# Column projections written half by half, two more weight tiles, and PSUM banks in turn for the delta heads

## The chip, the cores and the metric

The kernel runs on one core of a Trainium2 chip. Its engines are TensorE (PE in the profile; its weight loads are listed apart as PEld), VectorE (DVE), ScalarE (ACT), GpSimd (POOL) and SyncE (SP), which here issues the DMAs. Each engine works through its own instruction list in order and waits on semaphores. TensorE writes its results into PSUM, which has eight banks of 128 x 512 floats; ACT and DVE read them out from there. The metric is the device time of one execution in microseconds (us), the median of three: 2317.09 us before the change, with 2314.77 as the lowest and 2318.42 as the highest.

## The reference

Two transformer-like layers are applied in turn to x, 1024 tokens of 1024 features, in float32. Cut to what the change touches:

```python
# first layer
proj = einsum('bld,de->ble', rmsnorm(x), w_in)          # 1024 x 4112
attn = neighbourhood_attention(aq, ak, av) * silu(az)   # 8 heads of 64, a window of 8 x 16 tokens
qkv  = silu(depthwise_conv(dq, dk, dv))                 # 4 delta heads of 128, five taps along the tokens
dq, dk = l2norm(dq), l2norm(dk)
a_mat = strict(kb @ k^T) * decay + I                    # per chunk of 64 tokens, both directions
intra = (q @ k^T) * decay
# ... triangular solve, a scan over chunks with a state, gate, then x = x + [attn, delta] @ w_out
# second layer
proj = einsum('bsd,dc->bsc', rmsnorm(x), w_in_2)        # 1024 x 10240
out_a = stick_breaking_attention(q, k, v) * silu(sb_g)  # 8 heads of 128
out_b = rmsnorm(chunkwise_retention(rot(r_q), rot(r_k), r_v)) * silu(r_g)   # 4 heads of 256
merged = sigmoid(m_sb) * (out_a @ w_branch_sb) + sigmoid(m_ret) * (out_b @ w_branch_ret)
x = x + merged @ w_out_2
```

## The kernel before

Every large product is done as three matmuls in a rounded format (fp32r): the activations are held as a high part and a low part, the weights too, and high x high, low x high and high x low are added in PSUM. The weights come from DRAM in tiles of 128 rows. `split_unit` (line 60) loads one such tile (`raw`), and GpSimd makes the high part of it (L70) and the low part (L71); some loads of the stage with eight attention heads give every second tile to ACT and DVE. `load_units` does this for the eight tiles of a weight panel up to 512 columns wide. The split tiles (`wu`) live in the pool `wpool` of 10 buffers, so beside the eight of the panel in use two of the next panel fit.

Two forms of projection use a panel. `dense_tok` (L102 for its matmuls) puts tokens on the partitions: one accumulator `acc` per 128 tokens. `dense_col` (L112) puts 128 output features on the partitions and all 1024 tokens on the free axis; these need two accumulators of 512 tokens. It takes two banks at once and writes matmuls to the two halves in turn: for each of the eight weight tiles and each of the three passes one matmul per half, 48 in all (the framework regroups some of them, as far as its two banks allow). `dense_half` (L120) does one half alone, 24 matmuls into one bank; before, only the very last block of the program uses it. The accumulators come from pool `psA`, three banks called "a". The other five banks are "z" (two), "t", "o" and "p".

The stages, in order, with what they are called in the profile's times:

- up to 57 us: the first norm, the transposes and one `dense_tok`;
- 57 to 320 us, delta heads (loop at L296): for each of four heads three columns by `dense_col` (q, k, v), each read out by ACT into `pad` (L315), convolved by five DVE instructions (L318, L320) and put through Silu (L323). Then small products on TensorE: sums of squares (L330), transposes of k and v (L341, L351) and of the normalized k (L355), k k^T (L402) and q k^T (L417). Each has a fixed bank tag: "z", "z", "t", "o", "t", "p". The results are weighted on DVE (`N`, `IT`, `sct`) and leave for DRAM;
- 320 to 610 us, neighbourhood attention of eight heads, beside a triangular solver on DVE and POOL;
- 610 to 850 us, the scan over chunks and the product with `w_out`;
- 850 to 1440 us, eight heads of stick-breaking attention: `dense_tok` of the next head beside the attention of the present one, one `dense_col` per head for the gate;
- 1440 to 1960 us, retention, four heads: `ret_proj` makes q and k by four columns, rotates them on DVE and POOL (L1103 to L1108), makes v by `dense_tok` and the gate by two columns; `ret_chain` makes scores (L1151), weights `wT`, a transposed and scaled k called `kd` (L132, L1162, L1163), outputs (L1171, L1179) and states (L1192) chunk by chunk;
- 1960 us to the end: the rest of the merge logits, two branch products and the last product, all by `dense_col`.

The program is written with one pool-and-tile framework that orders the instructions itself (`schedule_with_timeline_sim=True`): it places an instruction on its engine's list when its own estimate says that its inputs and its buffer are ready. So the order in which lines stand in the source is not the order on an engine, and a change of buffers moves instructions of all engines. `tbank(tags)` (line 159) takes the next tag of a string, in turn, through one counter for the whole program.

Of the kernel before, what the change touches and what calls it, by code (L numbers as in the profile page):

```python
# [19 lines left out]
P = 128  # L20
T = 1024
NM = 8
NK = 8
# [13 lines left out]
def tile_kernel(ctx: ExitStack, tc: tile.TileContext, I: dict, out: bass.AP, dbg=None, stop=None):  # L37
    nc = tc.nc
# [7 lines left out]
    wraw = ctx.enter_context(tc.tile_pool(name="wraw", bufs=3))  # L46
    wpool = ctx.enter_context(tc.tile_pool(name="wpool", bufs=10))
    psA = ctx.enter_context(tc.tile_pool(name="psA", bufs=3, space=PSUM))
# [57 lines left out]

    def dense_col(hT, us, c0):
        accs = [bank("a") for _ in range(2)]
        for k in range(NK):
            for i, (a, b) in enumerate(((0, 0), (1, 0), (0, 1))):  # L110
                for half in range(2):
                    nc.tensor.matmul(accs[half], lhsT=us[k][:, b, c0:c0 + P], rhs=hT[a][:, k, half * 512:(half + 1) * 512],  # L112
                                     start=(k == 0 and i == 0), stop=(k == NK - 1 and i == 2))
        return accs

    def dense_half(hT, us, c0, half):
        acc = bank("a")
        for k in range(NK):
            for i, (a, b) in enumerate(((0, 0), (1, 0), (0, 1))):
                nc.tensor.matmul(acc, lhsT=us[k][:, b, c0:c0 + P], rhs=hT[a][:, k, half * 512:(half + 1) * 512],  # L120
                                 start=(k == 0 and i == 0), stop=(k == NK - 1 and i == 2))
        return acc

    def rsqrt_small(dst, src, mul, eps, eshape):
# [179 lines left out]
    for h in range(4):  # L304
# [22 lines left out]
        nc.scalar.activation(out=sq, in_=sT[0], func=AF.Square)  # L327
        pq = bank("z")
        for m in range(NM):
# [7 lines left out]
        for g in range(2):  # L337
            pk = bank("z")
            for j in range(4):
                m = g * 4 + j  # L340
                nc.tensor.transpose(pk[:, j * P:(j + 1) * P], sT[1][:, m * P:(m + 1) * P], ident)  # L341
            for j in range(4):
# [4 lines left out]
                                    in1=ks[:, g * 4:g * 4 + 4].unsqueeze(2).to_broadcast([P, 4, P]), op=ALU.mult)  # L347
            pv = bank("t")
            for j in range(4):
                m = g * 4 + j  # L350
                nc.tensor.transpose(pv[:, j * P:(j + 1) * P], sT[2][:, m * P:(m + 1) * P], ident)  # L351
            nc.scalar.copy(out=vt[:, g * 4:g * 4 + 4, :].rearrange("p m d -> p (m d)"), in_=pv)
            pk2 = bank("o")
            for j in range(4):
# [12 lines left out]
        for d in range(2):  # L367
# [27 lines left out]
            else:  # L395
                E2 = decay(gb, G, 1, True, "E1")
                nc.vector.tensor_tensor(out=E2, in0=E2, in1=bb, op=ALU.mult)
                for g in range(2):
                    pkk = bank("t")
                    for j in range(4):  # L400
# [12 lines left out]
                for g in range(2):  # L413
                    pkq = bank("p")
                    for j in range(4):
                        n = g * 4 + j
                        nc.tensor.matmul(pkq[:, j * P:(j + 1) * P], lhsT=kT[:, n * P:(n + 1) * P],  # L417
                                         rhs=sT[0][:, n * P:(n + 1) * P], start=True, stop=True)
                    for dd_, E in enumerate((E0, E1)):
                        IT = dn.tile([P, 4, P], F32, tag="IN", name="IT", bufs=2)  # L420
                        nc.vector.tensor_tensor(out=IT, in0=pkq.rearrange("p (n c) -> p n c", n=4),
                                                in1=E[:, g * 4:g * 4 + 4, :], op=ALU.mult)
                        nc.sync.dma_start(out=d_pk[dd_, g * 4:g * 4 + 4, :, 3, h, :].rearrange("n p c -> p n c"), in_=IT)
# [842 lines left out]
    for q in range(2):  # L1266
        us = load_units(I["w_out_2"], q * 512, 512)
        for b in range(4):
            last = 4 * q + b == 7
            for half, acc in enumerate(dense_col(mgT, us, b * P) if not last else (dense_half(mgT, us, b * P, x) for x in range(2))):  # L1270
                hs = slice(half * 512, half * 512 + 512)
# [76 lines left out]
```

## Time and profile before

| | |
|---|---|
| median of three runs | 2317.09 us |
| the profiled execution | 2316.85 us, its span from first to last instruction 2315.1 us |
| TensorE's mean granted clock | 0.984 of full speed |
| TensorE matmuls (PE) | busy 2182.2 us, 94% of the span, 12197 instructions |
| weight loads (PEld) | busy 1875.5 us, 81%, 12197 instructions |
| DVE, ACT, POOL | busy 1242.6, 879.1 and 1210.2 us |
| DMA | 249.25 MB, 108 GB/s |

The profile is one execution seen by the hardware profiler. "Busy" is the time in which an engine has an instruction running; overlapping instructions count once. Matmuls are pipelined, so one matmul's listed duration (about 0.39 us for 512 columns) is longer than the distance to the next. A view of waits names the engine and line that waited, what released it, the total, the number of times and the longest one. The granted clock is the share of TensorE's full 2.4 GHz that the chip allowed in a stretch: it is either 1.0 or 0.5 (1.2 GHz).

### The profile page before, as it was taken

What the parts mean: (1) busy time and instruction counts of PE and PEld (TensorE: products, weight loads), DVE (VectorE), ACT (ScalarE), POOL (GpSimd) and SP (SyncE); (2) the same over time, 40 slices, a digit from 0 to 9 for tenths busy, and PEclk for the clock granted to TensorE, in tenths of its full rate; (3) what the DMA queues carried; (4) which work ended last, traced back from release to release, by engine and by line L of the source; (5) the groups of instructions that cost most, each with busy time, mean ns of one, the idle gap of its engine ahead of it and who ended that gap; (6) DMA issues with size and microseconds to landing.
All of it is one profiled execution on the core that took longest, in us unless ns stands there. A gap on an engine that the chain in (4) does not pass through costs nothing.

```text
span 2315.1 us, 33643 instructions
## 1 busy us (share of the span) xinstructions
PE 2182.2 (94%) x12197; PEld 1875.5 (81%) x12197; DVE 1242.6 (54%) x2228; ACT 879.1 (38%) x2191; POOL 1210.2 (52%) x1435
## 2 busy tenths in 40 slices
PE   7998888899999988999999999999989999999999
PEld 7777877787898778988888888788878788788887
DVE  4688789844457555665566453327474744321221
ACT  5344434445544225565566544012222222321200
POOL 6667778762004345554565545536575754434531
PEclk9999999999999999999999999999999999999999
DMA  4266830054486431110111103221324333644433
GB/s 129 83 165 166 206 86 26 35 159 130 146 280 215 147 106 42 55 47 23 51 51 55 51 32 97 67 69 55 125 87 132 95 105 101 218 164 152 142 106 107
DMA packets 238791, 249.25 MB, mean 108 GB/s; under 512 B 40032, under 2 KB 173856, under 8 KB 238368
## 3 DMA queue, kind: packets, MB, share of 16 engines
q1 hardware_dynamic: 238624, 247.10, 34.0%
q8 instruction: 96, 1.57, 0.3%
q14 instruction: 71, 0.58, 0.1%
HBM read 171.51 MB, written 75.53 MB: 107 GB/s over the span
## 4 chain that ended last, share of the span: by engine, by line
PE 43%; POOL 7%; DVE 7%; issue 4%; DMA 3%; ACT 3%; SPq 0%; POOLq 0%; ACTq 0%
PE acc L112 26%; PE acc L102 9%; PE acc L859 3%; POOL wu L71 2%; DMA raw<-in_w_in_dram 2%; PE po L1063 2%; DVE A L1042 1%; POOL wu L70 1%; DVE A L1037 1%; POOL A L1047 1%; PE pt L1179 1%; POOL ss L126 1%; ACT A L1036 1%; DVE xo L909 1%; DVE kf L132 1%
## 5 line engine op out<-in xcount | busy, mean ns | idle before, releaser
L112 PE MATMUL acc<-h2h,wu 128*128 128x512 f32 x1504 | 460.5, 396 | 0.7 <-POOL wu L71 0.4
L102 PE MATMUL acc<-wu,h2h 128*128 128x384 f32 (+1 forms) x1536 | 374.5, 326 | 11.5 <-DVE v L1117 5.5
L71 POOL TENSOR_TENSOR wu<-raw,wu 128x512 fp32r<-128x512 f32 (+3 forms) x268 | 364.9, 1370 | 6.1
L70 POOL TENSOR_SCALAR wu<-raw 128x512 fp32r<-128x512 f32 (+3 forms) x268 | 206.3, 773 | 269.1 <-PE acc L112 187.9
L112 PEld LDWEIGHTS acc<-h2h,wu 128*128 128x128 f32 x1504 | 281.8, 188 | 65.2 <-POOL wu L71 0.8
L102 PEld LDWEIGHTS acc<-wu,h2h 128*128 128x128 f32 x1536 | 270.4, 192 | 18.4 <-DVE v L1117 6.3
L112 PE MATMUL acc<-h2l,wu 128*128 128x512 f32 x752 | 277.9, 395 | 0.0
L102 PE MATMUL acc<-wu,h2l 128*128 128x384 f32 (+1 forms) x768 | 248.2, 324 | 0.0
L102 PE MATMUL acc<-wu,h1hi 128*128 128x384 f32 (+2 forms) x768 | 192.2, 334 | 12.7 <-DVE kS L518 6.7
L112 PE MATMUL acc<-h1hi,wu 128*128 128x512 f32 x512 | 164.5, 409 | 7.3 <-ACT pad L315 3.7
L112 PEld LDWEIGHTS acc<-h2l,wu 128*128 128x128 f32 x752 | 141.3, 188 | 31.0
L102 PEld LDWEIGHTS acc<-wu,h1hi 128*128 128x128 f32 x768 | 137.3, 195 | 17.0 <-issue 8.0
L102 PEld LDWEIGHTS acc<-wu,h2l 128*128 128x128 f32 x768 | 147.5, 192 | 1.3
L1047 POOL TENSOR_TENSOR A<-Z,A 128x128 f32<-128x128 f32 (+2 forms) x96 | 111.3, 1165 | 66.3 <-DVE A L1042 48.4
L125 POOL TENSOR_SCALAR ss<-ss 128x2 f32<-128x2 f32 (+2 forms) x136 | 40.7, 300 | 200.4 <-ACT sq L983 144.0
L102 PE MATMUL acc<-wu,h1lo 128*128 128x384 f32 (+2 forms) x384 | 126.8, 333 | 0.0
L112 PEld LDWEIGHTS acc<-h1hi,wu 128*128 128x128 f32 x512 | 98.2, 194 | 32.3 <-ACT pad L315 5.4
L126 POOL TENSOR_TENSOR ss<-ss,mhalf 128x2 f32<-128x2 f32 (+2 forms) x136 | 113.5, 835 | 8.3
L112 PE MATMUL acc<-h1lo,wu 128*128 128x512 f32 x256 | 96.2, 405 | 0.0
L1037 DVE SCALAR_TENSOR_TENSOR A<-Z,A 128x128 f32<-128x128 f32 (+2 forms) x96 | 70.4, 742 | 42.7 <-ACT A L1036 41.8
L1063 PE MATMUL po<-wT,v 128*128 128x512 f32 (+3 forms) x288 | 76.2, 362 | 14.0 <-DVE wT L1061 11.0
L320 DVE SCALAR_TENSOR_TENSOR cv<-pad,c_conv_w,cv 128x1024 f32<-128x1024 f32 x48 | 76.6, 1597 | 1.1
(549 smaller groups left out, 4685.1 us busy)
## 6 DMA issues: line engine op xcount, KB each, us to landing
raw<-in_w_in_dram SPq DMA_DIRECT2D x192, 256.0 KB, 3.0
d_pk<-sct SPq DMA_DIRECT2D x24, 512.0 KB, 4.3
raw<-in_w_out_dram SPq DMA_DIRECT2D x40, 256.0 KB, 2.9
wsa<-d_pk SPq DMA_DIRECT2D x16, 512.0 KB, 6.1
wsb<-d_pk SPq DMA_DIRECT2D x16, 512.0 KB, 7.1
d_sg<-lg SPq DMA_DIRECT2D x32, 256.0 KB, 2.9
sg<-d_sg SPq DMA_DIRECT2D x32, 256.0 KB, 3.4
raw<-in_w_in_dram SPq DMA_DIRECT2D x32, 192.0 KB, 2.7
```

The lines of the kernel that those rows point to most:

```text
L70: nc.gpsimd.tensor_scalar(out=u[:, 0, :], in0=raw, scalar1=1.0, scalar2=0.0, op0=ALU.mult, op1=ALU.add)
L71: nc.gpsimd.tensor_tensor(out=u[:, 1, :], in0=raw, in1=f32(u[:, 0, :]), op=ALU.subtract)
L102: nc.tensor.matmul(acc[:, :n], lhsT=hT[a][:, k, m * P:(m + 1) * P], rhs=us[k][:, b, c0:c0 + n], start=(k == 0 and i == 0), stop=(k == NK - ...
L112: nc.tensor.matmul(accs[half], lhsT=us[k][:, b, c0:c0 + P], rhs=hT[a][:, k, half * 512:(half + 1) * 512], start=(k == 0 and i == 0), stop= ...
L125: nc.gpsimd.tensor_scalar(out=dst, in0=src, scalar1=mul, scalar2=eps, op0=ALU.mult, op1=ALU.add)
L126: nc.gpsimd.tensor_tensor(out=dst, in0=dst, in1=mhalf[:, :eshape], op=ALU.pow)
L132: nc.vector.transpose(out=dst[32 * b:32 * b + 32, :, :, 32 * a:32 * a + 32], in_=src[32 * a:32 * a + 32, :, :, 32 * b:32 * b + 32])
L320: nc.vector.scalar_tensor_tensor(out=cv, in0=pad[:, i:i + T], scalar=conv_w[:, blk, i:i + 1], in1=cv, op0=ALU.mult, op1=ALU.add)
L859: nc.tensor.matmul(acc, lhsT=us[k][:, y, (b % 4) * P:(b % 4 + 1) * P], rhs=token_set(mT[x][:, k, 0:T], s), start=(k == 0 and i == 0), stop ...
L1037: nc.vector.scalar_tensor_tensor(out=A[:, :w], in0=Z[:, :w], scalar=0.0, in1=A[:, :w], op0=ALU.max, op1=ALU.add)
L1047: nc.gpsimd.tensor_tensor(out=A[:, :w], in0=Z[:, :w], in1=A[:, :w], op=ALU.subtract)
L1063: nc.tensor.matmul(po[:, i0 * P:512], lhsT=v[a][:, c0 // P + kb, :], rhs=wT[b][:, :n], start=(diag and kb == 0 and x == 0), stop=(diag == ...
```

## The change

Three edits. `dense_col` becomes a generator that calls `dense_half` for the first 512 tokens and then for the second, so that the two accumulators are filled one after the other and each is taken from the three "a" banks only when its half begins; every user loops over it as before. `wpool` gets 12 buffers for 10. In the delta heads the six kinds of small product take the banks "z", "p", "t", "z", "o" in turn through `tbank` where they had a fixed one. The special case for the last block goes, since `dense_col` now does the same. Behind the edited functions all line numbers are smaller by four (L1171 becomes L1167).

```diff
-    wpool = ctx.enter_context(tc.tile_pool(name="wpool", bufs=10))
+    wpool = ctx.enter_context(tc.tile_pool(name="wpool", bufs=12))
...
-    def dense_col(hT, us, c0):
-        accs = [bank("a") for _ in range(2)]
-        for k in range(NK):
-            for i, (a, b) in enumerate(((0, 0), (1, 0), (0, 1))):
-                for half in range(2):
-                    nc.tensor.matmul(accs[half], lhsT=us[k][:, b, c0:c0 + P], rhs=hT[a][:, k, half * 512:(half + 1) * 512],
-                                     start=(k == 0 and i == 0), stop=(k == NK - 1 and i == 2))
-        return accs
...
+    def dense_col(hT, us, c0):
+
+        for half in range(2):
+            yield dense_half(hT, us, c0, half)
...
-        pq = bank("z")
+        pq = tbank("zptzo")
...
-            pk = bank("z")
+            pk = tbank("zptzo")
...
-            pv = bank("t")
+            pv = tbank("zptzo")
...
-            pk2 = bank("o")
+            pk2 = tbank("zptzo")
...
-                    pkk = bank("t")
+                    pkk = tbank("zptzo")
...
-                    pkq = bank("p")
+                    pkq = tbank("zptzo")
...
-            last = 4 * q + b == 7
-            for half, acc in enumerate(dense_col(mgT, us, b * P) if not last else (dense_half(mgT, us, b * P, x) for x in range(2))):
+            for half, acc in enumerate(dense_col(mgT, us, b * P)):
```

Where the instructions stand now is shown at three places. The first is TensorE's list at the start of the third column of the first delta head, with the buffers' numbers: acc_825 is the first half's accumulator and acc_826 the second's, wu_658 and wu_663 are the first two weight tiles, h1hi and h1lo the parts of the activations. Before:

```order
L112 MATMUL acc_825<-h1hi0_96,wu_658 128x512
L112 MATMUL acc_826<-h1hi0_96,wu_658 128x512
L112 MATMUL acc_825<-h1lo0_97,wu_658 128x512
L112 MATMUL acc_826<-h1lo0_97,wu_658 128x512
L112 MATMUL acc_825<-h1hi0_96,wu_658 128x512
L112 MATMUL acc_826<-h1hi0_96,wu_658 128x512
```

After, at the same place (dense_half's matmul is L111 there):

```order
L111 MATMUL acc_825<-h1hi0_96,wu_658 128x512
L111 MATMUL acc_825<-h1lo0_97,wu_658 128x512
L111 MATMUL acc_825<-h1hi0_96,wu_658 128x512
L111 MATMUL acc_825<-h1hi0_96,wu_663 128x512
L111 MATMUL acc_825<-h1lo0_97,wu_663 128x512
L111 MATMUL acc_825<-h1hi0_96,wu_663 128x512
```

The two halves alternated, so both ended within one matmul of each other; now the first half ends 24 matmuls ahead of the second.

The second place is TensorE's list in the first delta head where its small products stand: pt, pp, po and pz are banks, kT is the transposed k, s the convolved q. Before:

```order
L112 MATMUL acc<-h1hi_98,wu 128x512 x2
L355 MATMUL po<-ident,kt 128x128 x4
L402 MATMUL pt<-kT 128x128 x4
L417 MATMUL pp<-s,kT 128x128 x4
L112 MATMUL acc<-h1hi_98,wu 128x512 x2
L112 MATMUL acc<-h1lo_99,wu 128x512 x2
L112 MATMUL acc<-h1hi_98,wu 128x512 x4
```

After (L398 is k k^T, L413 is q k^T):

```order
L111 MATMUL acc<-h1lo_97,wu 128x512
L398 MATMUL pz<-kT 128x128 x4
L413 MATMUL pt<-s,kT 128x128
L398 MATMUL pp<-kT 128x128 x4
L413 MATMUL pt<-s,kT 128x128 x3
L413 MATMUL pz<-s,kT 128x128 x4
L111 MATMUL acc<-h1hi_96,wu 128x512 x2
```

Before, the second group of k k^T stood 18 rows further down and the second group of q k^T 55 rows further down, since each needs the one "t" or "p" bank again; after, both groups of both stand together.

The third place is POOL's list at the end of the first panel of the delta heads and the start of the second: wu_1059, 1064, 1069 and 1074 are the second head's first four weight tiles (the second head's first high part stands just ahead of the rows in both), E the decay of the first head, pad the convolution's input, dzt a gate. Before:

```order
L70 TENSOR_SCALAR wu_1064<-raw_1062 128x384
L71 TENSOR_TENSOR wu_1059<-raw_1057,wu_1059 128x384
L71 TENSOR_TENSOR wu_1064<-raw_1062,wu_1064 128x384
L312 MEMSET pad_696 128x2
L313 MEMSET pad_696 128x2
L312 MEMSET pad_759 128x2
L313 MEMSET pad_759 128x2
L386 AFFINE_SELECT E_957<-E_957 128x1024
L386 AFFINE_SELECT E_969<-E_969 128x1024
L70 TENSOR_SCALAR wu_1069<-raw_1067 128x384
L71 TENSOR_TENSOR wu_1069<-raw_1067,wu_1069 128x384
L70 TENSOR_SCALAR wu_1074<-raw_1072 128x384
```

After:

```order
L71 TENSOR_TENSOR wu_1064<-raw_1062,wu_1064 128x384
L70 TENSOR_SCALAR wu_1069<-raw_1067 128x384
L246 TENSOR_TENSOR dzt_386<-dzt_386,c_dn_norm_w_383 128x2048
L71 TENSOR_TENSOR wu_1069<-raw_1067,wu_1069 128x384
L70 TENSOR_SCALAR wu_1074<-raw_1072 128x384
L71 TENSOR_TENSOR wu_1074<-raw_1072,wu_1074 128x384
L308 MEMSET pad_696 128x2
L309 MEMSET pad_696 128x2
L308 MEMSET pad_759 128x2
L309 MEMSET pad_759 128x2
L382 AFFINE_SELECT E_957<-E_957 128x1024
L382 AFFINE_SELECT E_969<-E_969 128x1024
```

Four tiles of the second head now stand complete ahead of the two selections of E, where two stood before.

## Rows read from the trace of the kernel before

**Rows 1.** Busy time by engine, by stretch: us; PE, PEld, DVE, ACT, POOL; clock.

```profile
57.00:320.00 263.00, 233.77 (x1160) 197.79 (x1161) 209.13 (x227) 110.42 (x231) 191.60 (x187) 0.95 0.57 154
...
1440.00:1960.00 520.00, 494.12 (x2705) 424.07 (x2704) 272.13 (x443) 114.58 (x251) 299.75 (x302) 0.99 0.30 96
1960.00:2315.00 355.00, 351.07 (x1517) 283.05 (x1515) 80.46 (x101) 60.77 (x89) 140.15 (x132) 1.00 0.43 146
```

**Rows 2.** PE and PEld busy, clock; dense_col's matmuls (L112) alone.

```profile
2225.00:2295.00 70.00, 70.00 (x302) 56.40 (x301) 1.00 0.35 121
```

**Rows 3.** The same; dense_half's matmuls (L120) alone.

```profile
2301.00:2311.00 10.00, 10.00 (x44) 8.08 (x43) 1.00 0.29 105
```

**Rows 4.** Instructions in order, PE: start, us, line, tiles, idle before and releaser.

```profile
91.25 0.74 PE L112 MATMUL acc<-h1hi,wu 128*128 128x512 f32 x2 [2.10 <-POOL wu L71]
...
136.09 0.50 PE L112 MATMUL acc<-h1hi,wu 128*128 128x512 f32 x1 [1.88 <-ACT pad L315]
```

**Rows 5.** The same, ACT.

```profile
135.47 1.06 ACT L315 COPY pad<-acc 128x512 f32<-128x512 f32 x2
```

**Rows 6.** PE's waits, 57 to 320 us: total us, times, longest.

```profile
PE po L355 <- DVE kt L346: 5.0, 5, 3.3
PE acc L102 <- DVE kS L518: 4.5, 1, 4.5
PE acc L514 <- DVE kn L506: 3.9, 3, 2.7
PE acc L112 <- ACT pad L315: 3.7, 3, 1.9
PE acc L112 <- POOL wu L71: 3.1, 2, 2.1
PE acc L102 <- ACT pad L315: 2.9, 1, 2.9
...
PE acc L102 <- POOL wu L71: 1.4, 1, 1.4
```

**Rows 7.** The same, 1960 to 2315 us.

```profile
PE acc L112 <- ACT lg L956: 0.4, 1, 0.4
```

**Rows 8.** The same, 1440 to 1960 us.

```profile
PE acc L102 <- DVE v L1117: 5.5, 4, 3.2
...
PE pz L1151 <- POOL ro L1108: 3.4, 4, 1.2
...
PE acc L102 <- POOL wu L71: 2.7, 5, 0.9
```

**Rows 9.** Instructions in order, POOL, around 80 us, columns as in rows 4.

```profile
80.06 1.49 POOL L70 TENSOR_SCALAR wu<-raw 128x384 fp32r<-128x384 f32 x1
81.63 1.86 POOL L71 TENSOR_TENSOR wu<-raw,wu 128x384 fp32r<-128x384 f32 x1
```

**Rows 10.** Busy time by engine in two short stretches, columns as in rows 1.

```profile
92.90:96.30 3.40, 3.12 (x7) 2.48 (x8) 3.26 (x3) 0.00 (x0) 3.32 (x3) 0.50 0.30 81
...
1506.00:1509.40 3.40, 2.96 (x14) 2.96 (x15) 3.29 (x7) 1.03 (x2) 0.00 (x0) 0.50 0.22 74
```

**Rows 11.** DVE's waits, 84 to 260 us.

```profile
DVE cv L318 <- ACT pad L315: 2.6, 2, 2.1
...
DVE sct L430 <- ACT kT L356: 2.1, 2, 1.8
DVE rq L331 <- PE pz L330: 2.0, 1, 2.0
```

**Rows 12.** Instructions in order, DVE, around 1500 us.

```profile
1499.05 6.29 DVE L132 STREAM_TRANSPOSE kf<-ro 32x256 f32<-32x256 f32 x14
```

**Rows 13.** PE's waits, 850 to 1440 us.

```profile
PE acc L102 <- DVE sq L989: 3.1, 6, 0.8
```

**Rows 14.** Instructions in order, DVE, 68 to 90 us.

```profile
71.62 1.28 DVE L320 SCALAR_TENSOR_TENSOR cv<-pad,c_conv_w,cv 128x1024 f32<-128x1024 f32 x1
...
82.54 6.88 DVE L320 SCALAR_TENSOR_TENSOR cv<-pad,c_conv_w,cv 128x1024 f32<-128x1024 f32 x4
```

## The prediction

> **What bounds the kernel now.** I read the busy times stage by stage first, then TensorE's waits inside the stages that the change touches, then the instructions around the longest waits. TensorE is the engine to watch: from 1960 us to the end it is busy 351.07 of 355 us, in retention 494.12 of 520, in the delta heads 233.77 of 263 [rows 1]. So there is nearly nothing to win in the last stage and 29 us of idle TensorE in the delta heads, but there DVE too is busy 209.13 of 263 us [rows 1], and that will matter.
>
> The work of a column is unchanged: 48 matmuls. Does their rate depend on whether two banks are filled in turn or one? The alternating form runs 302 matmuls in 70.00 us, 0.232 us each [rows 2]. The last block of the program already has the new form: 44 in 10.00 us, 0.227 [rows 3]; a matmul cut by an edge counts whole, so both are the same 0.23. Weight loads are as many as matmuls in both and stay below them (56.40 us in 70.00 and 8.08 in 10.00). Term for the rate: 0.
>
> **Part by part.** *Halves one after the other.* What changes is how long a full accumulator may wait for its reader. Before, both halves of a column end together; the next column begins in the third bank. In four of the twelve columns of the delta heads TensorE's list puts 15 matmuls into it (15 x 0.232 = 3.5 us) ahead of the first into the second bank, in the others between 1 and 24. After, the half that just ended gets its bank asked back only after two more halves, 48 x 0.232 = 11.1 us. Where ACT is held up longer than 3.5 us, TensorE waits today: at 136.09 us for 1.88 us, while ACT was at other work and reached its two `pad` copies at 135.47 [rows 4, 5]. In the delta heads this wait is 3.7 us before columns and 2.9 us before the `dense_tok` behind them, 6.6 us [rows 6]. I expect all of it to go as a wait on a bank.
>
> In the last stage the same wait is 0.4 us [rows 7]: the scheduler already hides it there. Term: 0, bounds -0.4 and +1 (two reloads of a bank of 0.5 us, were each to show).
>
> *Twelve weight tiles.* TensorE waits for tiles 3.1 + 1.4 us in the delta heads [rows 6] and 2.7 us in retention [rows 8]. At 91.25 us it waited 2.10 us for the sixth tile of the second head [rows 4]. POOL's list now has two more tiles of that head ahead of the selections of E; at 1.49 + 1.86 us a tile [rows 9] each later tile comes some 6.7 us sooner, and only the eighth can still be late, by about 1 us. Against this, a panel's tiles now come free only in the last half column, not in the last column; with four tiles ahead, four remain to be made.
>
> *The clock.* A wait of about two microseconds or more costs again afterwards: the granted clock was 0.50, the 1.2 GHz level, for a stretch of 3.4 us from 92.90 us, behind the wait for the tile that ended at 91.25, and for another from 1506.00 us in retention [rows 4, 10]. There are four such stretches behind waits that the change touches: three in the delta heads (the other two behind waits on `pad`) and one in retention. Half the work of 3.4 us is 1.7 us each, 5.1 us in the delta heads.
>
> *Banks in turn.* Among TensorE's longer waits none is for one of these fixed banks [rows 6]; the scheduler had moved the second groups far down its list. What the turns give is that the groups stand earlier, so that DVE gets its inputs earlier.
>
> *Sum of the delta heads.* Upper end: 6.6 + 4.5 + 5.1 = 16.2 us saved. But TensorE's last waits there are for DVE: `kt` 5.0, `kS` 4.5, `kn` 3.9 us [rows 6]. If DVE comes no sooner, TensorE only arrives earlier and waits longer for these, and the gain is 0. Below nothing: the new list puts transposes of `kt` ahead of dense work in two heads; two more waits as long as the longest for `kt`, 3.3 us, cost 6.6. DVE itself can gain what it waits for drains and small products: 2.6 + 2.1 + 2.0 = 6.7 us [rows 11]. That is the row nearest to what decides, so I take -6, with ends -16.2 and +6.6.
>
> *Retention.* With halves, the rotated k of the first 512 tokens can start 24 x 0.232 = 5.6 us sooner. TensorE waits here for bank `acc` behind DVE's `v` 5.5 us, for the rotation 3.4, for weights 2.7 [rows 8], 11.6 us, and 1.7 us of slow clock follow the longest of them; upper end 13.3. DVE reached `v` late because it was in the transposes `kf`, 6.29 us for 14 of 16 [rows 12]; these start sooner now. Lower end: the new list puts head 0's first products on `wT` and `kd` right behind its scores; if `kd` is as late as now, its 6.29 us and 1.7 us of clock are paid there, +8. I take -5, the lead of 5.6 us seen once, in head 0, where rotation, `v` and weights all wait within a few microseconds; the later heads have other work in between.
>
> *Others.* In the stage of eight heads the order of TensorE's list is the same but for the columns; a column takes one bank of three where it took two, so the wait of `dense_tok` on `sq`, 3.1 us [rows 13], can shrink: -1, ends -3.1 and 0. Neighbourhood attention and scan: the list is shifted by a few small products both ways, 0, ends -2 and +3 (one wait like the longest for `kt`).
>
> Sum: -6 - 5 - 1 = -12 on the profiled execution's 2316.85 us gives 2305. That execution lies 0.24 us from the median, so the sum stands for the median too.
>
> **Rivals.** *DVE takes it all.* The waits on banks and tiles go, and TensorE stands as long before `kt`, `kn` and `kS`; retention's chain of states does the same. For it: DVE busy 80% of the delta heads [rows 1]. Against: DVE has 54 us of idle time there. What is left is 2 or 3 us: 2314. A convolution step on DVE took 1.28 us with POOL quiet and 1.72 (6.88 / 4) beside POOL's weight tiles [rows 9, 14], so packing the same work closer makes DVE slower. On this the Trainium skill, page "SBUF — State Buffer", section "Who interferes with whom", says that a DVE instruction with two SBUF inputs contends with a GpSimd instruction that reads SBUF; the trace agrees, and by that rule the gain of the delta heads would be lost first.
>
> *All of it comes.* Every wait counted goes with its slow stretch: 2317 - 16.2 - 13.3 - 1 = 2286; half way between it and 2305 is 2295. Against: such sums have never a single limiter.
>
> *Weights become the wait (slower).* Four tiles must be split between the release in the last half column (4.9 us before its end) and about 6.7 us into the next panel, 11.6 us, or 2.9 us a tile. POOL needs 1.49 + 1.86 = 3.35 us where DVE works beside it [rows 9]: 3.35 x 4 = 13.4, so 1.8 us late at each of some 12 loads of the delta heads and retention, 22 us, less 8 us of drained banks: 2331. It decides from 2.9 us a tile on. Against: TensorE's new list at panel ends still mixes the two halves where tiles are late, and POOL is idle 71 of 263 us in the delta heads.
>
> **How the numbers follow.** A measurement of this kernel tells 0.2%, 4.6 us, from no change: faster is below 2312.5, slower above 2321.7. My forecast, 2295 to 2312, has 0.52; all of it, below 2295, 0.10; DVE takes it, 2312 to 2321, 0.25; weights, above 2321, 0.13. So faster 0.62, same 0.25, slower 0.13. The likeliest case's own range is 2295 to 2312. The range of 8 in 10 is 2290 to 2323: it leaves out about 0.07 of the case that all comes and 0.11 of the one of the weights.
>
> **What would show it.** In the profile after, in the delta heads: no wait of TensorE on `pad`; the wait on weight tiles below 2 us; no 0.50 stretch at the places of 91, 136 and 232 us; the waits on `kt`, `kS`, `kn` no more than some 5 us longer. In retention: the wait of `acc` on `v` below 3 us, and no wait over 2 us on `kd` in head 0. The last 355 us unchanged within 2 us, with the same 0.232 us per matmul. The forecast is wrong if DVE-held waits of TensorE grow by what the others lose, or if waits on `wu` exceed today's 3.1 + 1.4 + 2.7 = 7.2 us.

## The result and the profile after

The changed kernel takes 2330.45 us (median of five runs, 2324.62 to 2333.95) against 2317.09: a ratio of 1.0059, 95% interval 1.0043 to 1.0075. It is slower by some 14 us where the forecast was 12 us faster; 2330 lies above the range of 2290 to 2323. The profiled execution is the fastest of the five, 2324.62 us, its span 2322.6 us, so the trace shows some 8 us of the loss and the other runs have more of it.

Where in the program? The last product of the eight-head stage on TensorE began at 1436.7 us before. After (first line below, the times near its end are its first and last start), and in a kernel with the tile edit alone, which is told further down (second line):

```profile
L1059 PE MATMUL po<-wT,v x288: 220/391/505, 927.1 to 1449.0; 128*128 128x512 f32 x80, 128*128 128x256 f32 x32, 128*128 128x384 f32 x16, 128*128 128x128 f32 x16
```

```profile
L1063 PE MATMUL po<-wT,v x288: 220/391/502, 916.8 to 1442.1; 128*128 128x512 f32 x80, 128*128 128x256 f32 x32, 128*128 128x384 f32 x16, 128*128 128x128 f32 x16
```

So 12.3 us are lost ahead of 1449 us, and as the span ends only 7.5 us later, 4.8 us come back behind it. Nearly all of the loss is there early: if the columns of TensorE's matmuls are summed up in the order of their starts, the sum that the kernel before had reached at 320 us is reached 11.7 us later. The stages after, by busy time (columns as in [rows 1]), the first and last line in answer to those of [rows 1], and two stretches at half clock in answer to [rows 10]:

```profile
57.00:320.00 263.00, 231.36 (x1101) 192.92 (x1101) 197.18 (x202) 104.18 (x213) 175.48 (x167) 0.92 0.55 149
...
1440.00:1960.00 520.00, 495.85 (x2726) 426.30 (x2725) 269.09 (x443) 116.96 (x250) 297.59 (x299) 0.99 0.29 95
1960.00:2315.00 355.00, 355.00 (x1543) 287.24 (x1542) 84.31 (x103) 62.77 (x94) 147.61 (x138) 1.00 0.43 147
...
135.20:142.00 6.80, 5.33 (x11) 3.30 (x12) 6.80 (x5) 1.97 (x3) 6.80 (x5) 0.50 0.92 278
...
244.40:254.60 10.20, 9.81 (x37) 9.31 (x37) 10.20 (x9) 5.99 (x15) 9.75 (x8) 0.50 1.02 272
```

In the delta heads TensorE starts 1101 matmuls in the same 263 us that held 1160, and the mean granted clock is 0.92 for 0.95: 0.03 x 263 = 8 us of full-speed time less. TensorE's own idle time grew by 2.4 us only, from 29.2 to 31.6, so most of the loss of this stage is the clock. DVE and POOL are both less busy, 197.18 for 209.13 and 175.48 for 191.60: neither of them took over the bound. The waits of TensorE there, in answer to [rows 6]:

```profile
PE acc L510 <- DVE kn L502: 5.4, 2, 3.9
PE acc L111 <- POOL wu L71: 3.9, 7, 1.2
PE pz L347 <- ACT s L319: 3.6, 1, 3.6
PE acc L111 <- POOL wu L70: 3.3, 4, 1.0
PE pz L351 <- DVE kt L342: 3.1, 1, 3.1
PE pt L337 <- ACT s L319: 2.9, 1, 2.9
...
PE acc L102 <- POOL wu L71: 2.5, 2, 2.0
PE po L326 <- ACT sq L323: 1.7, 1, 1.7
```

No wait on `pad` is left, as forecast. In its place stand transposes that wait for the convolved `s` (3.6 + 2.9 us), and waits on tiles of 9.7 us (3.9 + 3.3 + 2.5) where there were 4.5. Before, the only wait for `s` of this view was

```profile
PE pt L351 <- ACT s L323: 2.4, 2, 1.8
```

The waits for `kt` are no longer than before.

### The profile page after: what moved, and what is told of

Read it like the earlier page. It is cut to its first block, busy times and chain, and to the rows that moved or that the text cites. A ratio compares the mean times of both kernels' runs of the same rounds, so it can differ in the third digit from the quotient of the medians.

```text
span 2322.6 us, 33626 instructions
## 1 busy us (share of the span) xinstructions
PE 2189.9 (94%) x12197; PEld 1880.7 (81%) x12197; DVE 1243.0 (54%) x2228; ACT 882.9 (38%) x2191; POOL 1213.9 (52%) x1435
## 4 chain that ended last, share of the span: by engine, by line
PE 56%; DVE 13%; POOL 12%; issue 7%; DMA 6%; ACT 4%; SPq 1%; POOLq 0%; ACTq 0%; DVEq 0%
PE acc L111 27%; PE acc L102 13%; DMA raw<-in_w_in_dram 3%; POOL wu L71 3%; POOL wu L70 3%; PE acc L855 2%; DVE A L1038 2%; PE po L1059 1%; PE pz L548 1%; DVE X L461 1%; DVE svt L459 1%; PE pt L565 1%; POOL ss L122 1%; POOL A L1043 1%; DVE cv L316 1%
## 5 line engine op out<-in xcount | busy, mean ns | idle before, releaser
L111 PE MATMUL acc<-h2h,wu 128*128 128x512 f32 x1504 | 479.6, 396 | 1.1 <-POOL wu L71 0.8
L111 PEld LDWEIGHTS acc<-h2h,wu 128*128 128x128 f32 x1504 | 281.5, 188 | 66.2 <-POOL wu L71 2.8
L111 PE MATMUL acc<-h2l,wu 128*128 128x512 f32 x752 | 296.0, 395 | 0.0
L111 PE MATMUL acc<-h1hi,wu 128*128 128x512 f32 x512 | 173.2, 414 | 8.0 <-POOL wu L71 3.9
L111 PEld LDWEIGHTS acc<-h2l,wu 128*128 128x128 f32 x752 | 141.6, 188 | 31.6
L111 PEld LDWEIGHTS acc<-h1hi,wu 128*128 128x128 f32 x512 | 100.2, 198 | 36.4 <-POOL wu L71 8.0
L111 PE MATMUL acc<-h1lo,wu 128*128 128x512 f32 x256 | 105.8, 413 | 0.0
L111 PE MATMUL acc<-oah,wu 128*128 128x512 f32 x256 | 80.3, 395 | 0.0
```

## The experiments

Ratios are to the kernel before, run on the same chip at the same time; 0.1% is 2.3 us. "T" is 12 tiles, "B" banks in turn, "H" half by half.

| kernel | median us | ratio | interval |
|---|---|---|---|
| changed (T, B, H) | 2330.45 | 1.0059 | 1.0043 to 1.0075 |
| only T | 2307.74 | 0.9950 | 0.9933 to 0.9966 |
| only B | 2341.01 | 1.0094 | 1.0077 to 1.0110 |
| T, H (fixed banks) | 2320.95 | 1.0005 | 0.9994 to 1.0016 |
| T, B | 2326.30 | 1.0029 | 1.0019 to 1.0038 |
| B, H (ten tiles) | 2334.80 | 1.0067 | 1.0051 to 1.0082 |
| H in delta heads only | 2329.08 | 1.0039 | 1.0024 to 1.0053 |
| T, H in delta heads only | 2316.33 | 0.9975 | 0.9962 to 0.9989 |
| H behind the delta heads only | 2321.81 | 1.0011 | 1.0000 to 1.0021 |
| T, H behind the delta heads only | 2317.50 | 0.9989 | 0.9977 to 1.0002 |
| the same with B | 2326.10 | 1.0030 | 1.0018 to 1.0043 |
| tags exchanged | 2317.47 | 0.9994 | 0.9984 to 1.0003 |

**First four: tiles or banks?** The edits, in the order of the expectations. Alternating columns in the delta heads of the changed kernel (dense_alt is the old dense_col):

```diff
-            for half, acc in enumerate(dense_col(hT, us, b * P)):
+            for half, acc in enumerate(dense_alt(hT, us, b * P)):
```

> The changed kernel, but the twelve columns of the delta heads are again written with the two halves in turn; all later columns stay half by half, 12 weight tiles and banks in turn stay. Theory A (tiles): one half alone walks through the eight weight tiles of a panel in 24 matmuls, 5.6 us, where both halves in turn take 11.1 us, and gives each tile back only in the last 5.6 us; GpSimd, at about 3.4 us a tile, falls behind, and the waits on tiles in the delta heads (9.7 us after, 4.5 before) and the half-clock stretches behind them are the loss. It expects waits on tiles at or below 4.5 us there, a mean clock of 0.95 in 57 to 320 us (0.92 after), and, as the later stages keep their 5 us gain, 2310 to 2316 us. Theory B (banks): the turns pull small products ahead of dense work, TensorE waits for s, kt and sq, 14.3 us after against 7.4 before, and that is the loss. It expects no change against the changed kernel: 2326 to 2332 us, with those waits still near 14 us.

Measured: 2326.1 us, the lower end of B's range, though by the ratio 0.29% better than the changed kernel; waits on tiles 4.5 us, but the clock stayed at 0.92. Theory A falls as the sole cause. Fixed banks in the changed kernel:

```diff
-        pq = tbank("zptzo")
+        pq = bank("z")
...
```

> The changed kernel, but the six kinds of small product of the delta heads have their fixed banks again; halves everywhere and 12 tiles stay. Theory A (tiles): the loss stays, 2326 to 2332 us, waits on tiles in the delta heads near 10 us. Theory B (banks): the loss goes, 2310 to 2317 us, and TensorE's waits on s, kt and sq in the delta heads fall from 14 to about 7 us.

Measured: 2320.95 us. Of the slowdown 0.54% (12.5 us) goes with the turns, so theory B holds in the main, though the time is above its 2310 to 2317; the waits on tiles, which A expected to stay, fell to 4.1 us. Ten tiles, and halves in the delta heads alone:

```diff
-    wpool = ctx.enter_context(tc.tile_pool(name="wpool", bufs=12))
+    wpool = ctx.enter_context(tc.tile_pool(name="wpool", bufs=10))
```

> The changed kernel with 10 weight tiles for 12; halves and banks in turn stay. Theory A (tiles): with two tiles of the next panel ready for four, two more tiles of each of the three later panels of the delta heads must be made while they are wanted; the waits on tiles grow by up to 2 x 3.4 us at each panel, so 2335 to 2350 us. Theory B (banks): tiles don't matter, 2328 to 2333 us.

> The kernel before with one edit: the twelve columns of the delta heads half by half; 10 tiles, fixed banks, later columns with the halves in turn. Theory A (tiles): the loss of the delta heads without the gain of the later stages, and with fewer tiles: 2325 to 2345 us, waits on tiles in 57 to 320 us above 10 us. Theory B (banks): halves do no harm, 2312 to 2319 us.

Measured: 2334.8 us, just between the two theories, and 2329.08 us. The intervals of the first and of the changed kernel overlap, so tiles are worth little beside the two other edits; halves alone in the delta heads do harm (0.39%), against B, with 7.8 us of waits on tiles, fewer than A wanted.

**Each edit alone, and halves without the delta heads.**

```diff
-    wpool = ctx.enter_context(tc.tile_pool(name="wpool", bufs=10))
+    wpool = ctx.enter_context(tc.tile_pool(name="wpool", bufs=12))
```

> The kernel before with one edit: 12 weight tiles. Waits on tiles are 4.5 us in the delta heads and 3.1 us in retention before. Theory A (tiles): without halves 10 tiles are nearly enough; the waits on tiles fall by some 3 us and a stretch at half clock goes with them: 2311 to 2317 us. Rival (any change of the list disturbs a list that happened to fit): waits on other inputs take their place, 2317 to 2325 us.

> The kernel before with one edit: the six kinds of small product of the delta heads on banks in turn; 10 tiles, halves in turn everywhere. The first runs gave both theories a part: with fixed banks the changed kernel lost only 3 us against before, with alternating columns in the delta heads 8, and in every one of them more time at half clock came with the loss. Theory B (banks), now: the turns let the framework write the transposes of s ahead of dense work, TensorE then stands at them for ACT's s (about 13 us in the first 500 us with turns and alternating columns, 5 before), and a stretch at half clock follows each of these waits. It expects 2323 to 2329 us from the turns alone, and waits on s above 9 us in 57 to 320 us. Theory C (turns hurt only together with halves or 12 tiles, through POOL's work): 2314 to 2320 us.

> The changed kernel with the delta heads of before: columns with the halves in turn and fixed banks there, and 10 weight tiles; half by half from the stage of neighbourhood attention on. If the later stages' gain (5 us between 1440 and 1960 us in the trace after) is the halves' own: 2310 to 2314 us. Rival: that gain only gives back what the delta heads lost, since DVE and POOL had more time there: then none without the loss, 2315 to 2319 us.

> The same with 12 weight tiles: delta heads as in before, half by half behind them. If tiles and later halves add: 2307 to 2313 us, the fastest of all. Rival (a list that no longer fits): 2316 to 2324 us.

Measured: tiles alone 0.9950, more gain than either theory said; it beats both kernels and stands at the end as the best version. Turns alone 1.0094, 22 us, more harm than B said, and not by the waits that it named: those on `s` were 4.3 us, not above 9. Halves behind the delta heads gain nothing with 10 tiles and take back 0.39% beside 12. One edit put on top of the other makes a ladder: tiles -0.50%, halves beside them +0.55%, turns beside both +0.54%. That the sum is +0.59%, the measured change, is so by construction, and another order gives other sizes: halves cost 0.30% beside tiles and turns, and beside turns with ten tiles they take 0.27% off (1.0067 against 1.0094, the intervals just overlap). Halves in the whole program with ten tiles and fixed banks were not run.

GpSimd's list in the kernel with turns alone, where the third head's tiles begin (start, us, line, tiles, idle before and releaser):

```profile
124.38 1.54 POOL L386 TENSOR_SCALAR_AFFINE_SELECT E<-E 128x1024 f32<-128x1024 f32 x1 [8.43 <-DVE E L385]
125.90 2.42 POOL L430 TENSOR_TENSOR sct<-s,G 128x1024 f32<-128x1024 f32 x1
128.30 2.94 POOL L70 TENSOR_SCALAR wu<-raw 128x384 fp32r<-128x384 f32 x2
```

and in the kernel before:

```profile
123.63 1.28 POOL L70 TENSOR_SCALAR wu<-raw 128x384 fp32r<-128x384 f32 x1 [8.11 <-PE acc L112]
...
131.81 2.08 POOL L386 TENSOR_SCALAR_AFFINE_SELECT E<-E 128x1024 f32<-128x1024 f32 x1
133.86 2.36 POOL L430 TENSOR_TENSOR sct<-s,G 128x1024 f32<-128x1024 f32 x1
```

Before, GpSimd waits for TensorE to give the buffer back and makes the tile at once. With turns it stands 8.43 us for DVE's E, since the work on E and `sct` was written ahead, and the first tile comes 4.7 us later. Waits on tiles in the delta heads are 12.3 us there (9.3 + 2.6 + 0.4).

**Is that the whole harm of the turns?** Turns beside 12 tiles, the products alone in turn, a control (its edit is shown), and halves without retention's q and k:

```diff
-            pv = bank("t")
+            pv = bank("o")
...
-            pk2 = bank("o")
+            pk2 = bank("t")
...
-                    pkk = bank("t")
+                    pkk = bank("o")
```

> The kernel before with two of the three edits: banks in turn and 12 tiles, no halves. The turns alone cost 21 us, the tiles alone gave 12. Theory D (the turns do their harm through GpSimd): with products earlier, GpSimd's selection of E and its multiplication for sct stand in its list ahead of the next panel's weight tiles, and TensorE waits for tiles, 11.9 us in the delta heads with turns alone, 4.5 before. Two more tiles in hand take most of that away: waits on tiles below 4 us, and the turns cost 9 us or less beside 12 tiles: 2308 to 2317 us. Theory B (the turns do their harm through waits on s, kt and kS): the 21 us stay, 2325 to 2331 us.

> 12 tiles, no halves, and only k k^T and q k^T on banks in turn; the transposes and the sums of squares keep their fixed banks. These two products feed DVE and then GpSimd's work, the transposes feed ACT and DVE. Theory D: the harm of the turns comes through these two: as with all six in turn, 2310 to 2317 us, against 2307.7 with none. Theory B: it comes from transposes that stand too early: 2306 to 2309 us.

> The kernel before with fixed banks, but two tags exchanged in the delta heads: transposes of v and k k^T on o, the transposes of the normalized k on t. As many products per bank as before, and nothing else is changed: a measure of what a change without a purpose does through the framework's order. If the list of before is an ordinary one: within 5 us of before, 2313 to 2323 us. If it is one that happened to fit, and any other is worse: 2323 to 2335 us.

> 12 tiles, delta heads as in before, half by half elsewhere but not in the q and k columns of retention. With these too half by half the time was 2317.5 us, with 12 tiles and no halves 2307.7. Theory E: the 10 us between the two come from retention: with halves in q and k the framework writes the first outputs of head 0 (the product of wT and v) earlier, TensorE stands there 3.0 us for ACT's v, and a stretch at half clock follows. Without halves there that wait is gone and the time is 2306 to 2311 us. Rival: the halves of the gates or of the logits cost it, then 2315 to 2320 us.

Measured: 2326.3 us (1.0029): with tiles in hand the waits on them fall to 2.7 us, and the turns still cost 0.79%, 18 us. Theory D is a small part only; the time is in B's range. The two products alone: 2315.5 us (0.9984, interval 0.9973 to 0.9995), in D's range, but only 0.34% above tiles alone. The control: 0.9994, so this exchange of tags without a purpose moves the time by less than 0.2%. It is one such exchange; that no other would cost what the turns cost is not shown. Without halves in q and k: 2312.06 us (0.9965, 0.9952 to 0.9977), half way; theory E has half at most.

So what stands on DVE? Its list in the second head, tiles alone: one column's convolution, L318 and four L320:

```profile
120.04 0.75 DVE L318 TENSOR_SCALAR cv<-pad,c_conv_w 128x1024 f32<-128x1024 f32 x1
120.82 2.73 DVE L320 SCALAR_TENSOR_TENSOR cv<-pad,c_conv_w,cv 128x1024 f32<-128x1024 f32 x2
123.47 1.28 DVE L406 SCALAR_TENSOR_TENSOR N<-pt,E 128x512 f32<-128x512 f32 x2
124.67 1.31 DVE L320 SCALAR_TENSOR_TENSOR cv<-pad,c_conv_w,cv 128x1024 f32<-128x1024 f32 x1
...
127.35 2.04 DVE L320 SCALAR_TENSOR_TENSOR cv<-pad,c_conv_w,cv 128x1024 f32<-128x1024 f32 x1
```

and with turns beside 12 tiles:

```profile
121.42 0.74 DVE L318 TENSOR_SCALAR cv<-pad,c_conv_w 128x1024 f32<-128x1024 f32 x1
123.79 0.69 DVE L421 TENSOR_TENSOR IT<-pt,E 128x512 f32<-128x512 f32 x1 [1.63 <-DMA d_N<-N]
124.40 2.19 DVE L320 SCALAR_TENSOR_TENSOR cv<-pad,c_conv_w,cv 128x1024 f32<-128x1024 f32 x1
...
130.40 0.68 DVE L421 TENSOR_TENSOR IT<-pz,E 128x512 f32<-128x512 f32 x1
131.00 1.91 DVE L320 SCALAR_TENSOR_TENSOR cv<-pad,c_conv_w,cv 128x1024 f32<-128x1024 f32 x1
...
135.93 2.10 DVE L320 SCALAR_TENSOR_TENSOR cv<-pad,c_conv_w,cv 128x1024 f32<-128x1024 f32 x1
```

The same convolution takes from 120.04 to 129.39 us in the one and from 121.42 to 138.03 in the other. Since the groups of k k^T and q k^T now follow each other on TensorE, their readers stand one after the other on DVE, between the convolution's steps; and as N and IT share two buffers, DVE stands for a store (1.63 us) with the convolution behind it. TensorE's next wait, 2.4 us until 140.57, is for this `s`. That this is the price is not shown, though. With tiles alone TensorE stands 3.5 us for `pad` shortly before, and the next convolution starts only 1.4 us sooner. With turns:

```profile
138.56 1.47 DVE L318 TENSOR_SCALAR cv<-pad,c_conv_w 128x1024 f32<-128x1024 f32 x1
...
140.57 0.77 PE L341 MATMUL pz<-ident,s 128*128 128x128 f32 x5 [2.37 <-ACT s L323]
```

and with tiles alone:

```profile
136.66 0.79 PE L112 MATMUL acc<-h1hi,wu 128*128 128x512 f32 x1 [3.53 <-ACT pad L315]
...
137.13 1.53 DVE L318 TENSOR_SCALAR cv<-pad,c_conv_w 128x1024 f32<-128x1024 f32 x1 [0.27 <-ACT pad L315]
```

**The link.** Transposes alone in turn; four buffers for N and IT, with turns and with fixed banks; halves in retention's q and k alone:

```diff
-                        N = dn.tile([P, 4, P], F32, tag="IN", name="N", bufs=2)
+                        N = dn.tile([P, 4, P], F32, tag="IN", name="N", bufs=4)
...
-                        IT = dn.tile([P, 4, P], F32, tag="IN", name="IT", bufs=2)
+                        IT = dn.tile([P, 4, P], F32, tag="IN", name="IT", bufs=4)
```

> 12 tiles, no halves, and only the transposes of k, v and the normalized k on banks in turn; k k^T, q k^T and the sums of squares keep their fixed banks. All six in turn gave 2326 us beside 12 tiles, the two products alone 2315.5, none 2307.7. Theory G1 (the readers of the two products crowd between a column's convolution steps on DVE and hold the end of the delta heads back): the transposes alone cost little, 2306 to 2311 us, and the solver's first step on DVE begins near 293 us as with none (305 with all in turn). Theory G2 (the transposes stand earlier, so DVE's multiplication for kt stands earlier in its list and DVE waits for GpSimd's ks, 9.8 us with all in turn, 3.3 with none): the rest of the cost is here, 2315 to 2320 us, with that wait near 9 us.

> Banks in turn, 12 tiles, no halves, and four buffers for N and IT where there are two. With two, DVE waits 6.4 us in the delta heads for the stores of N and IT, in front of convolution steps; with fixed banks 0.3 us of N and IT waits on stores are named among the long ones. Theory G3 (this wait is the link): 2315 to 2320 us against 2326.3. If the link is elsewhere: 2322 to 2329 us.

> 12 tiles, fixed banks, no halves, and four buffers for N and IT. The partner of the run before: with fixed banks these stores are hardly waited for, so no change is expected, 2305 to 2311 us. If it is faster than 2305 us it beats both kernels further.

> 12 tiles, fixed banks, and half by half in retention's q and k columns alone. Theory E (a half that is done early lets the framework write head 0's first outputs ahead, where TensorE then waits 3 us for ACT's v and loses clock): 2311 to 2316 us, against 2307.7 without. If those columns half by half do no harm of their own: 2305 to 2310 us.

| beside 12 tiles, no halves unless named | median us | ratio | interval |
|---|---|---|---|
| transposes in turn | 2330.33 | 1.0043 | 1.0025 to 1.0061 |
| all in turn, four buffers | 2313.18 | 0.9968 | 0.9954 to 0.9983 |
| fixed banks, four buffers | 2307.73 | 0.9943 | 0.9924 to 0.9962 |
| H in retention's q and k | 2308.19 | 0.9947 | 0.9926 to 0.9968 |

The transposes alone cost as much as all six in turn (+0.93%): G1 falls. G2 has the place (DVE waits 7.8 us for GpSimd's `ks` in the delta heads, 3.3 with fixed banks), and less than half of the size: 2330 is above its 2315 to 2320. Four buffers take 0.61% (14 us) off with turns, more than G3 said, and nothing with fixed banks (-0.07%, within the intervals). DVE's waits for these stores between 84 and 300 us, with turns and two buffers:

```profile
DVE N L406 <- DMA d_N<-N: 3.4, 3, 2.4
...
DVE IT L421 <- DMA d_N<-N: 1.6, 1, 1.6
DVE IT L421 <- DMA d_pk<-IT: 1.4, 2, 0.8
```

and with four:

```profile
DVE IT L421 <- DMA d_N<-N: 1.1, 2, 0.9
```

With fixed banks and two buffers they are 2.3 us (1.7 + 0.4 + 0.2), more than the 0.3 that I had written. So 5.3 us of waits on DVE went, and 14 us of time. The two buffers are a part of the cause, but the stand at the store does not explain the cost of the turns. The transposes alone in turn cost 0.93%, with fewer of these waits than fixed banks have:

```profile
DVE N L406 <- DMA d_N<-N: 1.3, 1, 1.3
...
DVE IT L421 <- DMA d_N<-N: 0.7, 1, 0.7
```

The products alone have 5.2 us of them (4.1 + 0.8 + 0.3) and cost 0.34%. Four buffers beside the transposes alone were not run, and four buffers let the framework reorder, too.

What the cost does go with is the clock. The mean granted clock, as the median of all executions of a kernel, was 0.982 with tiles alone, 0.979 with the products in turn, 0.976 with all in turn and 0.975 with the transposes in turn; with all in turn and four buffers it was between 0.978 and 0.979, and with fixed banks and four buffers, which cost nothing, 0.980. The kernel before, run beside them, had 0.981 or 0.982. The step from 0.982 to 0.976 is 0.006 x 2317 = 14 us of full-speed time, of the 18 that the turns cost beside 12 tiles. So by this estimate most of the price is time at 1.2 GHz. Which waits brought TensorE there is not shown.

Halves in q and k alone did no harm that the time can tell, against theory E. Its wait is there all the same (waits of TensorE, 1440 to 1560 us, with these halves; L1175 there is L1171 of before):

```profile
PE pt L1175 <- ACT v L1120: 2.9, 1, 2.9
PE acc L102 <- DVE v L1121: 1.4, 1, 1.4
```

without them:

```profile
PE acc L102 <- DVE v L1117: 1.3, 1, 1.3
```

An interval of 0.2% to either side cannot exclude the few us that this would cost.

**The same in the changed kernel, and the rest of the halves.**

> The changed kernel with four buffers for N and IT where there are two; all three edits stay. Banks in turn beside 12 tiles cost 18.6 us with two such buffers and 5.5 with four. Theory G3 (DVE standing for the stores of N and IT, in front of convolution steps, is what makes the turns dear): in the changed kernel this wait is 5.3 us between 84 and 300 us, and without it the time is 2316 to 2322 us against 2330.5. If that holds only without halves: 2326 to 2332 us.

> 12 tiles, fixed banks, half by half in the delta heads alone. Theory A (a half alone asks for the tiles of a panel in half the time): with 10 tiles this edit cost 9 us, with 12 the waits on tiles in the delta heads stay below 3 us and the cost is 4 us or less: 2308 to 2312 us, against 2307.7 with 12 tiles and no halves. Theory H (the halves do harm of another kind, through the order on DVE and ACT): 2314 to 2320 us, with waits on tiles below 3 us all the same.

Measured: four buffers in the changed kernel 2325.32 us, 1.0013 (1.0001 to 1.0024); the runs of before beside it had a median of 2323.0, so by the ratio it is 0.46%, 10.7 us, better than the changed kernel, though its time is above the expected 2322. That is nearly the 12.5 us that the turns cost there; but four buffers with halves and fixed banks were not run, so not all of it need belong to the turns. In the trace the waits on these stores fell from 5.3 to 0.9 us, and TensorE's waits on tiles in the delta heads rose from 9.7 to 16.6 us. Halves in the delta heads beside 12 tiles: 0.9975, 0.25% (5.8 us) above tiles alone. Waits on `pad` are gone there (5.2 us with tiles alone), those on tiles small (1.0 + 0.5 us, and none named with tiles alone), and in their place TensorE waits for DVE:

```profile
245.45 1.11 PE L345 MATMUL pz<-ident,s 128*128 128x128 f32 x4 [4.18 <-DVE rq L335]
```

The reader that frees this bank stands on DVE behind a step of the convolution:

```profile
243.56 1.75 DVE L324 SCALAR_TENSOR_TENSOR cv<-pad,c_conv_w,cv 128x1024 f32<-128x1024 f32 x1
245.24 0.15 DVE L335 COPY rq<-pz 128x8 f32<-128x8 f32 x1
```

It takes 0.15 us and ends TensorE's wait of 4.18. Theory H is right about the kind of harm at this place. On the size neither is: 5.8 us lie between A's 4 at most and H's 6 at least, and the interval reaches into both.

## Why the prediction was wrong

- **Rate of matmuls, last stage:** right. 302 matmuls in 70.00 us again, and no wait of TensorE named from 1960 us on; the 0.4 us of [rows 7] is gone. The 0.5 us for the reload of a bank, in the upper bound, is shown by no run.
- **Halves one after the other:** a step that failed. The wait on the bank went as said, 6.6 us to none [rows 6]. That it is won was wrong: halves cost 0.55% beside 12 tiles. In the delta heads (0.25%) TensorE meets DVE's reader of another bank. The larger part, 0.39% behind them, is not settled: halves in q and k alone cost nothing that can be told, halves elsewhere 0.15%, and these don't add up. By the traces, from the last product of the eight-head stage to the end, the kernel with tiles alone gains 10.9 us on the kernel before, 8.6 with halves in q and k as well, 8.7 with halves elsewhere, and 3.4 with both.
- **Twelve tiles:** mis-sized. I gave them part of 4.5 us in the delta heads and of 2.7 in retention, and they are worth 0.50%, 11.6 us. In the trace with tiles alone the gain stands in the last two stages: that execution ran 5.4 us later than before at 1436.7 us and ended 5.5 us earlier. Its waits on tiles and rotation are gone from retention and that on `v` fell from 5.5 us [rows 8] to 2.5, while those on `kd` and `ot` rose from 3.2 and 4.3 us:

```profile
PE po L1192 <- ACT kd L1162: 7.1, 3, 3.8
PE pt L1171 <- DVE ot L1186: 6.9, 6, 1.9
PE acc L102 <- DVE v L1117: 2.5, 4, 1.3
```

- **Banks in turn:** the other step that failed. I costed them at nothing on their own: "What the turns give is that the groups stand earlier, so that DVE gets its inputs earlier." Earlier they stand, but DVE, ACT and POOL work in order too: what reads the products moved ahead of convolution steps, of `kt` and of tiles. Price 12.5 us in the changed kernel, 22 us alone. The price is shown by the edits; which of these moves makes it is not, and no single wait named here accounts for it. I had read the idle 54 us of DVE as room; it was not room at the place.
- **The clock:** a term with the wrong sign. I counted 5.1 us as won in the delta heads, and some 8 us more were lost; with it the stage, for which I took -6 with +6.6 as the worst end, lost 11.7 us. The three stretches that I wanted away are still there or longer: 94.20 to 97.60 us in place of 92.90 to 96.30, 135.20 to 142.00 in place of 137.30 to 140.70, 244.40 to 254.60 in place of 232.90 to 236.30.
- **Sum of retention:** -5 was forecast, and 4.8 us came back behind 1449 us. The cause that I gave, the lead of the first half, is not it: the tiles give more than that alone, and no kernel with halves added to it.
- **Rivals:** the one of the weights gave 2331 us, next to what was measured, but not by its mechanism: waits on tiles rose by 5.2 us, not 22, in retention they fell, and with fixed banks they stood at 4.1 us beside halves. The sign of a wrong forecast that I had named did come: waits on tiles of 10.5 us (9.7 + 0.8), above 7.2. "DVE takes it all" has the right kind of cause, and stopped at no gain; it had no way to a loss, since it counted only waits that move, not readers that push other work back. One reading in it was wrong: at the step of 1.28 us [rows 14] POOL was not quiet, it had a selection of E from 71.78 us on, for 2.07 us. Beside that selection the step was as short as the one at 68.78 us, where POOL did stand still (1.28 us), so the slowing to 1.72 us belongs to the weight tiles.

The Trainium skill, page "Perfetto Trace Analysis", section "Matmuls", says that independent matmul groups should rotate through different PSUM banks so that ACT and DVE empty one while the next is filled. Here turns cost 0.94% alone, 0.79% beside 12 tiles and 0.25% where N and IT had four buffers (0.9968 against 0.9943): the measurement decides. None of TensorE's longer waits had been for one of these banks [rows 6].

## What to carry to other kernels

A freed bank or a shorter wait on one engine moves the readers on every other in-order list: before counting it as won, look at what those lists now put in front, at the smallest pool that the readers share (here two buffers for N and IT), and at the granted clock over several executions. Take a bundle apart before keeping it: one of the three edits gave 0.5%, and the other two, put on top of it, took that twice. The best version is the kernel before with 12 weight tiles alone, 2307.74 us (0.9950); with four buffers for N and IT as well it is the same, 2307.73.

## What the runs showed of the hardware

Several short waits were followed by half clock as one long one is. In the trace after, TensorE's waits on tiles ahead of and in the stretch from 135.20 to 142.00 us were these, none as long as the two microseconds that I took to be the price of entry (a last one, 0.30 us, ended at 139.54):

```profile
132.66 0.50 PE L111 MATMUL acc<-h1hi,wu 128*128 128x512 f32 x1 [0.61 <-POOL wu L70]
...
133.74 0.50 PE L111 MATMUL acc<-h1hi,wu 128*128 128x512 f32 x1 [0.35 <-POOL wu L71]
...
135.20 0.80 PE L111 MATMUL acc<-h1hi,wu 128*128 128x512 f32 x1 [0.95 <-POOL wu L70]
...
137.59 1.22 PE L111 MATMUL acc<-h1hi,wu 128*128 128x512 f32 x2 [1.17 <-POOL wu L71]
```

Nor was every wait of two microseconds followed by half clock. In the kernel before, the clock was 1.00 from 374.20 to 384.20 us, right behind this one:

```profile
374.20 0.60 PE L102 MATMUL acc<-wu,h1hi 128*128 128x384 f32 x2 [2.20 <-DVE kS L518]
```

And one list of instructions does not have one clock: five executions of the changed kernel ran at mean clocks of 0.981, 0.980, 0.977, 0.974 and 0.974 and took 2324.62, 2328.48, 2330.45, 2333.14 and 2333.95 us. A difference of 0.2% needs many runs, and one trace may be the luckiest of them.
